# Sixteen FFN blocks by seven products in place of fourteen, sums of x in place, and another order at the end, in a two-layer decoder kernel

## The chip, the cores and the metric

The kernel runs on one core of one Trainium2 chip. The metric is the device time of one execution in microseconds, as the median of several runs. TensorE (PE in the rows, with PEld for its weight loads), VectorE (DVE), ScalarE (ACT) and GpSimd (POOL) each take their own instructions in order; SyncE (SP) issues the loads and stores.

## The reference

```python
D_MODEL, SEQ, D_FF = 1024, 512, 2752

def swiglu(h, w_gate, w_up, w_down):
    return (jax.nn.silu(h @ w_gate) * (h @ w_up)) @ w_down

for layer in range(2):
    x = x + 0.5 * swiglu(rmsnorm(x, ffn1_norm[layer]), ffn1 weights of the layer)
    h = rmsnorm(x, mix_norm[layer])
    if layer == 0:
        x = x + parallel_s5_stickbreak(h, ...)
    else:
        x = x + short_conv_mixer(h, ...)
    x = x + 0.5 * swiglu(rmsnorm(x, ffn2_norm[layer]), ffn2 weights of the layer)
return rmsnorm(x, final_norm)
```

All is float32. The four FFNs, numbered 0 to 3, are most of the work. The mixers are not touched by the change.

## The kernel before, in words

x lies transposed in eight tiles of 128 rows (features) by 512 columns (sequence). TensorE multiplies float32 by three products in a shorter format: each operand is split into an upper part ("hi", a cast on ScalarE) and a lower part ("lo", a subtraction on VectorE), and hi·hi, lo·hi and hi·lo are added (`mm3`, lines 309 to 311).

**Weights.** They are units of 128 x 1024 in an order fixed by the list of steps. A unit is loaded to one of three "raw" buffers, cast to "whi" (`cut_hi`, L212) and completed with "wlo" (`cut_lo`, L218); `refill` then issues the load three units on. `drive` runs the steps: for a unit it first calls `advance`, which cuts the unit that is two ahead, then issues the unit's products and what follows them (`after`). A unit with `split_before` skips `advance`. So the order of the calls is the order in each engine's queue.

**An FFN** has 21 blocks of 128 hidden columns and a tail of 64. It goes in three parts ("thirds"): the blocks of a part are computed, and then the down products of these blocks, in eight units (dt = 0 to 7), are added to x (L547). A plain block is two units (gate and up) over the eight tiles of x, 24 matmuls of 512 columns each. Its evacuation is, for the gate, t (L489), the silu s on ScalarE (L491) and s times rb (L492); for the up unit, the product (L501), its cast "hhi" (L502) and its lower part "hlo" (L503). rb is the reciprocal root of the norm. The tail block's lines are 512 to 520.

**Seven products.** In the second and third part of FFNs 1, 2 and 3 a block is computed by seven products of half size in place of eight, in the manner of Strassen and Winograd: gate and up weights, in halves of the 1024 features, against x in halves of features and sequence. This takes 84 matmuls of 256 columns (`seven_products`, L681), sums of the weights (`mate_pieces`, L279 to L284, "s" with parts "shi" and "slo") and sums of x. For x, `seven_x` (L615) forms "xn", x times norm times rb, two operations for each i of 0 to 3. Before, this follows blocks 3 to 6, and the sums and casts stand beside the down units: `seven_sums` (L633 to L640) makes four sums in scratch tiles "t", casts them ("thi") and casts parts of xn ("bhi"); `seven_lower` (L648 to L652) makes the lower parts "tlo" and "blo". With tail, the first part has 7 blocks and the tail, the others 7 each. FFN 0 is plain throughout.

**The end.** The last part of FFN 3 has its own function, `last_down`: the down units run twice, once for each half of the sequence (256 columns), 16 units in all. After a unit: x is updated (L764), and on ScalarE squared for the final norm (L773) and scaled (L774), and the squares are added (L776). During the second half, the first half's root is computed (`first_sums`, `norm_diag`, `first_bcast`) and its rows are stored.

Of the kernel before, what the change touches and what calls it, by code (L numbers as in the profile page):

```python
# [8 lines left out]
F32 = mybir.dt.float32  # L9
F32R = mybir.dt.float32r  # L10
I32 = mybir.dt.int32
AF = mybir.ActivationFunctionType
ALU = mybir.AluOpType
# [8 lines left out]
TAIL = 21  # L22
PLAIN_THIRDS = [list(range(0, 8)), list(range(8, 15)), list(range(15, 22))]
SEVEN_THIRDS = [list(range(0, 7)) + [TAIL], list(range(7, 14)), list(range(14, 21))]
SEVEN = (1, 2, 3)
# [118 lines left out]
class Trunk:  # L144
# [321 lines left out]
    def ffn(self, n, nxt):  # L466

        st = self
# [86 lines left out]

        for third in range(3):
# [7 lines left out]
            for f in [] if seven else sorted(thirds[third], key=lambda f: (f != TAIL or third == 0, f if f != TAIL else 4.5)):  # L564
                keep = []
                if f == TAIL:
                    st.steps.append(Unit(gu[n, 2 * f], 1024, st.over_x("A", keep), evac_tail(keep)))
                    continue
                g, u = evac_gate(keep, f), evac_up(keep, f)
                if f == 0:  # L570
                    early, keep0 = [g, u], keep
                    g = u = None
                    if n == st.first_ffn:
                        g, u = (lambda r=r: [st.feed_sq(st.first_norm, k) for k in r] for r in (range(4), range(4, 8)))
                elif f == 1:
                    def ug(g=g, u=u, keep=keep):
                        st.norm_bcast()
                        for kp, (gg, uu) in ((keep0, early), (keep, (g, u))):
                            pu = kp.pop()
                            gg()  # L580
                            kp.append(pu)
                            uu()
                    g, u = st.norm_sums, ug
                pair = [Unit(gu[n, 2 * f], 1024, st.over_x("A", keep), g), Unit(gu[n, 2 * f + 1], 1024, st.over_x("A", keep), u)]
                if f == 0 and n == st.first_ffn:
                    pair[0].products = lambda u, p=pair, k=keep: st.over_x_two("A", p, [k, k])
                    pair[1].products = lambda u: None
                st.steps += pair
                if n in SEVEN and 3 <= f < 7:
                    st.steps.append(lambda i=f - 3: st.seven_x(n, i))  # L590
# [26 lines left out]

    def seven_parts(self, dt):

        sums, lower = {0: (0, 1), 2: (2,), 3: (3,)}, {1: 0, 2: 1, 4: 2, 5: 3}  # L620
        return [lambda: self.seven_lower(lower[dt])] * (dt in lower) + [
            lambda i=i: self.seven_sums(i) for i in sums.get(dt, ())]

    def seven_sums(self, i):


        nc, v, x = self.nc, self.nc.vector, self.xn[i]
        b11, b12, b21, b22 = (x[:, c:c + 256] for c in range(0, 1024, 256))
        t = self.fp.tile([128, 512], F32, tag="t", name="t12", bufs=2), self.fp.tile([128, 512], F32, tag="s", name="t34", bufs=2)
        l, r = slice(0, 256), slice(256, 512)  # L630
        hi = [self.xgp.tile([128, 512], F32R, tag="xhi", name="thi") for _ in range(2)]
        b = self.sp7.tile([128, 768], F32R, tag="bhi", name="bhi", bufs=4)
        v.tensor_tensor(t[0][:, l], b12, b11, ALU.subtract)  # L633
        nc.scalar.copy(b[:, 0:256], b11)
        v.tensor_tensor(t[0][:, r], b22, t[0][:, l], ALU.subtract)
        nc.scalar.copy(hi[0], t[0])
        v.tensor_tensor(t[1][:, l], b22, b12, ALU.subtract)
        v.tensor_tensor(t[1][:, r], b21, t[0][:, r], ALU.subtract)
        nc.scalar.copy(hi[1], t[1])
        nc.scalar.copy(b[:, 256:768], x[:, 512:1024])  # L640
        self.t7[i], self.b7[i] = [t, hi], [b]

    def seven_lower(self, i):
        v, x = self.nc.vector, self.xn[i]
        t, hi = self.t7[i]
        lo = [self.xgp.tile([128, 512], F32R, tag="xlo", name="tlo") for _ in range(2)]
        for a, h, o in zip(t, hi, lo):
            v.tensor_tensor(o, a, h.bitcast(F32), ALU.subtract)  # L648
# [4 lines left out]
        self.t7[i], self.b7[i] = (hi, lo), (b, o)  # L653
# [6 lines left out]
    def seven_products(self, f, u):  # L660
# [31 lines left out]
        t1, t2, t3, t4 = (total(j) for j in range(4))  # L692
# [46 lines left out]
    def last_down(self, units):  # L739
# [20 lines left out]

        def after(dt, h):
            c = slice(h * H, h * H + H)
            x = st.x[dt][:, c]
            v.scalar_tensor_tensor(x, ps[dt, h], 0.5, x, ALU.mult, ALU.add)  # L764
# [10 lines left out]
            if 0 < dt < NK - 1:  # L775
                v.tensor_tensor(st.acc[:, c], st.acc[:, c], sq, ALU.add)  # L776

# [57 lines left out]
        extra = {0: [first_sums], 1: [lambda: st.norm_diag(2)], 2: [first_bcast]}  # L835
        for k in range(NK):
            extra.setdefault(3 + k // 2, []).append(lambda k=k: first_out(k))
        for h in range(2):
            for dt, u in enumerate(units[h]):
                u.products = lambda u, dt=dt, h=h: products(u, dt, h)  # L840
                todo = [lambda dt=dt, h=h: after(dt, h)]
                if h:
                    todo = extra.get(dt, []) + todo if dt == 0 else todo + extra.get(dt, [])
# [1104 lines left out]
```

## Time and profile before

| | |
|---|---|
| median of 3 runs | 1835.75 us (1835.69 to 1835.79) |
| profiled execution, its own time | 1837.11 us |
| its span, first to last instruction | 1835.4 us |
| granted TensorE clock, mean | 0.995 |
| busy: PE, PEld | 99%, 86% |
| busy: DVE, ACT, POOL | 71%, 40%, 6% |
| moved by DMA | 201.64 MB, mean 110 GB/s |

The rows shown later come from the profiled execution; its own time stands beside its span because the time around the span is not in any row. Busy time of PE is counted from instructions that overlap, so for what one matmul takes, look at the time of a stage and the number of its matmuls. A mean share says nothing of a single stage: the stages have different limits.

### The profile page before, as it was taken

Reading aid. Unit: us, or ns where it says so; the run is one execution under the profiler, and the core shown is the slowest. Engines: PE = TensorE matmul, PEld = TensorE weight load, DVE = VectorE, ACT = ScalarE, POOL = GpSimd, SP = SyncE. Lnnn points to the kernel's source line nnn. Section 1 sums busy time; section 2 is a strip of 40 time slices with the busy share of each in tenths; the row PEclk is TensorE's granted clock in tenths of the full one; section 3 lists DMA queues with packets and bytes.
Section 4 is the critical chain, followed back from the end, with each engine's and each line's share of the span. In section 5 each row is a group of like instructions: output and inputs, shape, how many; then the busy total and the mean of one; then the engine's idle time right before and its main releaser. Section 6 shows DMA issues by size and latency. Waiting matters only on the chain.

```text
span 1835.4 us, 25692 instructions
## 1 busy us (share of the span) xinstructions
PE 1808.5 (99%) x10006; PEld 1575.2 (86%) x10006; DVE 1299.5 (71%) x2157; ACT 741.4 (40%) x1117; POOL 116.5 (6%) x238
## 2 busy tenths in 40 slices
PE   9999999999989999999999999999999999999997
PEld 8887888888877788999988899898888888898997
DVE  6757777656787567967855689596655556895975
ACT  5322323334786334534443344244222333452444
POOL 0290000110000200000010000001100100000001
PEclk9999999999989999999999999999999999999999
DMA  4334444456411233332332333333333223333334
GB/s 162 122 98 139 122 131 145 134 169 214 144 47 47 81 104 92 115 100 96 108 103 89 95 111 98 98 114 94 95 101 104 92 86 99 104 102 105 103 105 127
DMA packets 82457, 201.64 MB, mean 110 GB/s; under 512 B 20816, under 2 KB 31072, under 8 KB 82336
## 3 DMA queue, kind: packets, MB, share of 16 engines
q1 hardware_dynamic: 82160, 199.97, 35.1%
q8 instruction: 78, 1.28, 0.3%
q14 instruction: 43, 0.35, 0.1%
q10 hardware_dynamic: 144, 0.03, 0.0%
q0 software_dynamic: 32, 0.01, 0.0%
HBM read 184.12 MB, written 12.58 MB: 107 GB/s over the span
## 4 chain that ended last, share of the span: by engine, by line
PE 87%; DVE 4%; POOL 3%; ACT 3%; issue 2%; DMA 1%; SPq 0%; DVEq 0%; POOLq 0%; ACTq 0%
PE ps_A L681 23%; PE ps_A L309 11%; PE ps_A L310 11%; PE ps_A L311 11%; PE ps_mm L309 8%; PE ps_mm L310 8%; PE ps_mm L311 8%; DVE wlo L218 1%; ACT whi L212 1%; PE ps_mm L1653 1%; PE ps_mm L1655 1%; PE ps_mm L1654 1%; PE ps_A L1248 0%; PE ps_A L1250 0%; PE ps_A L1249 0%
## 5 line engine op out<-in xcount | busy, mean ns | idle before, releaser
L218 DVE TENSOR_TENSOR wlo<-raw,whi 128x1024 fp32r<-128x1024 f32 (+1 forms) x290 | 355.8, 1227 | 131.9 <-ACT whi L212 131.4
L212 ACT CAST whi<-raw 128x1024 fp32r<-128x1024 f32 (+1 forms) x290 | 295.0, 1020 | 267.5 <-PE ps_mm L311 120.5
L309 PE MATMUL ps_A<-xhi,whi 128*128 128x512 f32 x896 | 350.5, 391 | 0.0
L310 PE MATMUL ps_A<-xhi,wlo 128*128 128x512 f32 x896 | 349.1, 390 | 1.4 <-DVE wlo L218 1.4
L311 PE MATMUL ps_A<-xlo,whi 128*128 128x512 f32 x896 | 348.9, 389 | 0.1
L309 PE MATMUL ps_mm<-hhi,whi 128*128 128x512 f32 (+1 forms) x672 | 256.7, 382 | 1.1 <-DVE x L764 1.1
L310 PE MATMUL ps_mm<-hhi,wlo 128*128 128x512 f32 (+1 forms) x672 | 256.3, 381 | 0.4 <-DVE wlo L218 0.4
L311 PE MATMUL ps_mm<-hlo,whi 128*128 128x512 f32 (+1 forms) x672 | 256.1, 381 | 0.0
L310 PEld LDWEIGHTS ps_A<-xhi,wlo 128*128 128x128 f32 x896 | 168.4, 188 | 36.9 <-DVE wlo L218 2.3
L309 PEld LDWEIGHTS ps_A<-xhi,whi 128*128 128x128 f32 x896 | 168.4, 188 | 35.6 <-issue 0.8
L311 PEld LDWEIGHTS ps_A<-xlo,whi 128*128 128x128 f32 x896 | 168.3, 188 | 35.7 <-DVE xlo L367 0.5
L309 PEld LDWEIGHTS ps_mm<-hhi,whi 128*128 128x128 f32 x672 | 127.1, 189 | 25.5 <-issue 1.7
L310 PEld LDWEIGHTS ps_mm<-hhi,wlo 128*128 128x128 f32 x672 | 127.2, 189 | 24.4 <-DVE wlo L218 0.6
L311 PEld LDWEIGHTS ps_mm<-hlo,whi 128*128 128x128 f32 x672 | 127.0, 189 | 24.0
L681 PE MATMUL ps_A<-thi,shi 128*128 128x256 f32 x504 | 142.6, 283 | 0.0
L681 PE MATMUL ps_A<-thi,slo 128*128 128x256 f32 x504 | 142.6, 283 | 0.0
L681 PE MATMUL ps_A<-tlo,shi 128*128 128x256 f32 x504 | 142.6, 283 | 0.0
L547 DVE SCALAR_TENSOR_TENSOR x<-ps_mm,x 128x512 f32<-128x512 f32 x88 | 60.4, 689 | 76.9 <-PE ps_mm L311 72.7
L269 DVE TENSOR_TENSOR slo<-s,shi 128x512 fp32r<-128x512 f32 (+1 forms) x126 | 107.7, 863 | 1.6
L681 PEld LDWEIGHTS ps_A<-thi,shi 128*128 128x128 f32 x504 | 96.8, 192 | 0.0
L681 PEld LDWEIGHTS ps_A<-thi,slo 128*128 128x128 f32 x504 | 96.8, 192 | 0.0
L681 PEld LDWEIGHTS ps_A<-tlo,shi 128*128 128x128 f32 x504 | 96.8, 192 | 0.0
(396 smaller groups left out, 3315.7 us busy)
## 6 DMA issues: line engine op xcount, KB each, us to landing
raw<-gu SPq DMA_DIRECT2D x170, 512.0 KB, 3.5
raw<-dn SPq DMA_DIRECT2D x96, 448.0 KB, 3.3
raw<-sci SPq DMA_DIRECT2D x24, 512.0 KB, 3.5
raw<-ab SPq DMA_DIRECT2D x16, 512.0 KB, 3.6
raw<-dn SPq DMA_DIRECT2D x8, 512.0 KB, 3.6
raw<-abo SPq DMA_DIRECT2D x8, 512.0 KB, 3.5
raw<-sco SPq DMA_DIRECT2D x8, 512.0 KB, 3.4
x<-xT SPq DMA_DIRECT2D x8, 256.0 KB, 5.1
```

The source lines that it names most:

```text
L212: self.nc.scalar.copy(u.hi[:, : u.cols], u.raw[:, : u.cols])
L218: (engine or self.nc.vector).tensor_tensor(u.lo[:, :c], u.raw[:, :c], u.hi[:, :c].bitcast(F32), ALU.subtract)
L269: v.tensor_tensor(u.s_lo[i][:, c], s[i][:, c], u.s_hi[i][:, c].bitcast(F32), ALU.subtract)
L309: nc.tensor.matmul(ps, whi, xhi, start=start and i == 0, stop=False)
L310: nc.tensor.matmul(ps, wlo, xhi, start=False, stop=False)
L311: nc.tensor.matmul(ps, whi, xlo, start=False, stop=stop and i == n - 1)
L547: nc.vector.scalar_tensor_tensor(x, keep[0], 0.5, x, ALU.mult, ALU.add)
L681: nc.tensor.matmul(ps, a, m, start=first and k == 0 and n == 0, stop=k == 3 and n == 2, skip_group_check=True)
L1653: nc.tensor.matmul(X["ps"], u.hi[:, c], hi, start=k == 0, stop=False)
L1654: nc.tensor.matmul(X["ps"], u.lo[:, c], hi, start=False, stop=False)
L1655: nc.tensor.matmul(X["ps"], u.hi[:, c], lo, start=False, stop=k == 3)
```

## The change

Three things are done together.

1. The parts of FFNs 1, 2 and 3 become 5 blocks and the tail, 8, and 8. So 16 blocks are computed by seven products, and the depths of the down units become 17, 24 and 24 matmuls in place of 23, 21 and 21. The end's 16 units get 24 matmuls of 256 columns in place of 21, and 512 KB of weights in place of 448.
2. `seven_x` now also casts the parts of xn ("bhi") on ScalarE, and is called after the units (2, gate), (2, up), (3, up) and (4, gate). The sums are made in place in xn, with "blo" ahead of them, after the tail, (3, gate), (4, up) and the first down unit. The casts "thi" and the lower parts "tlo" stay beside the down units. The tail moves between blocks 2 and 3.
3. In `last_down`, the cast of a unit's weights is issued ahead of the products two units before it; after the products come the update of x, then the lower part and the load, then square and scaling. The root's steps stand ahead of the update.

```diff
-SEVEN_THIRDS = [list(range(0, 7)) + [TAIL], list(range(7, 14)), list(range(14, 21))]
+SEVEN_THIRDS = [list(range(0, 5)) + [TAIL], list(range(5, 13)), list(range(13, 21))]
...
+        def seven_x(f, j):
+            if n not in SEVEN:
+                return []
+            x, t = (lambda i: [lambda: st.seven_x(n, i)]), (lambda i: [lambda: st.seven_sums(i)])
+            return {(2, 0): x(0), (2, 1): x(1), (TAIL, 0): t(0), (3, 0): t(1), (3, 1): x(2), (4, 0): x(3), (4, 1): t(2)}.get((f, j), [])
...
-            for f in [] if seven else sorted(thirds[third], key=lambda f: (f != TAIL or third == 0, f if f != TAIL else 4.5)):
+            for f in [] if seven else sorted(thirds[third], key=lambda f: (f != TAIL or third == 0, f if f != TAIL else 2.5)):
...
+                    st.steps += seven_x(f, 0)
...
-                st.steps += pair
-                if n in SEVEN and 3 <= f < 7:
-                    st.steps.append(lambda i=f - 3: st.seven_x(n, i))
+                for j in range(2):
+                    st.steps.append(pair[j])
+                    st.steps += seven_x(f, j)
...
+        b = self.sp7.tile([128, 768], F32R, tag="bhi", name="bhi", bufs=4)
+        self.nc.scalar.copy(b[:, 0:256], self.xn[i][:, 0:256])
+        self.nc.scalar.copy(b[:, 256:768], self.xn[i][:, 512:1024])
+        self.b7[i] = [b]
 
     def seven_sums(self, i):
...
         v.tensor_tensor(o[:, 0:256], x[:, 0:256], b[:, 0:256].bitcast(F32), ALU.subtract)
         v.tensor_tensor(o[:, 256:768], x[:, 512:1024], b[:, 256:768].bitcast(F32), ALU.subtract)
-        self.t7[i], self.b7[i] = (hi, lo), (b, o)
+        self.b7[i] = (b, o)
+        q11, q12, q21, q22 = (x[:, c:c + 256] for c in range(0, 1024, 256))
+        v.tensor_tensor(q11, q12, q11, ALU.subtract)
+        v.tensor_tensor(q12, q22, q12, ALU.subtract)
+        v.tensor_tensor(q22, q22, q11, ALU.subtract)
+        v.tensor_tensor(q21, q21, q22, ALU.subtract)
+
+    def seven_parts(self, dt):
+        return [lambda: self.seven_sums(3)] * (dt == 0) + [lambda: self.seven_lower(dt - 1)] * (1 <= dt <= 4) + [
+            lambda: self.seven_upper(dt)] * (dt < 4)
+
+    def seven_upper(self, i):
+        hi = [self.xgp.tile([128, 512], F32R, tag="xhi", name="thi") for _ in range(2)]
+        for j in range(2):
+            self.nc.scalar.copy(hi[j], self.xn[i][:, j * 512:(j + 1) * 512])
+        self.t7[i] = hi
+
+    def seven_lower(self, i):
+        hi = self.t7[i]
+        lo = [self.xgp.tile([128, 512], F32R, tag="xlo", name="tlo") for _ in range(2)]
+        for j in range(2):
+            self.nc.vector.tensor_tensor(lo[j], self.xn[i][:, j * 512:(j + 1) * 512], hi[j].bitcast(F32), ALU.subtract)
+        self.t7[i] = (hi, lo)
...
-        t1, t2, t3, t4 = (total(j) for j in range(4))
+        t1, t3, t4, t2 = (total(j) for j in range(4))
...
+        def first_part(u):
+            if st.split < len(st.units):
+                st.cut_hi(st.split)
+
+        def second_part():
+            n = st.split
+            if n < len(st.units):
+                st.cut_lo(n)
+                st.refill(n)
...
-        extra = {0: [first_sums], 1: [lambda: st.norm_diag(2)], 2: [first_bcast]}
+        extra = {}
...
+        early = {0: [first_sums], 1: [lambda: st.norm_diag(2)], 2: [first_bcast]}
...
-                u.products = lambda u, dt=dt, h=h: products(u, dt, h)
-                todo = [lambda dt=dt, h=h: after(dt, h)]
-                if h:
-                    todo = extra.get(dt, []) + todo if dt == 0 else todo + extra.get(dt, [])
+                u.split_before = True
+                u.products = lambda u, dt=dt, h=h: (first_part(u), products(u, dt, h))
+                todo = early.get(dt, []) * h + [lambda dt=dt, h=h: update(dt, h), second_part, lambda dt=dt, h=h: after(dt, h)]
+                todo += extra.get(dt, []) * h
```

How this moves the instructions is seen at three places. The first is ScalarE in FFN 1, from the silu of block 2's gate on. Before:

```order
L491 ACTIVATE s<-t 128x512
L212 CAST whi<-raw 128x1024
L502 CAST hhi<-s 128x512
L212 CAST whi<-raw 128x1024
L491 ACTIVATE s<-t 128x512
```

Now:

```order
L491 ACTIVATE s<-t 128x512
L626 CAST bhi<-xn 128x256
L627 CAST bhi<-xn 128x512
L212 CAST whi<-raw 128x1024
L502 CAST hhi<-s 128x512
L626 CAST bhi<-xn 128x256
L627 CAST bhi<-xn 128x512
L212 CAST whi<-raw 128x1024
L513 ACTIVATE s<-t 64x512
```

Two casts of xn now stand ahead of each weight cast, and the tail's silu follows block 2. The second place is VectorE over the same steps. Before:

```order
L489 TENSOR_TENSOR t<-ps_A,rb 128x512
L492 TENSOR_TENSOR s<-s,rb 128x512
L218 TENSOR_TENSOR wlo<-raw,whi 128x1024
L501 TENSOR_TENSOR s<-ps_A,s 128x512
L503 TENSOR_TENSOR hlo<-s,hhi 128x512
L218 TENSOR_TENSOR wlo<-raw,whi 128x1024
```

Now, and on to the tail's second lower part, the sum made after it and the weights behind that:

```order
L489 TENSOR_TENSOR t<-ps_A,rb 128x512
L492 TENSOR_TENSOR s<-s,rb 128x512
L623 SCALAR_TENSOR_TENSOR xn<-x_82,norms,rb 128x512
L623 SCALAR_TENSOR_TENSOR xn<-x_93,norms,rb 128x512
L218 TENSOR_TENSOR wlo<-raw,whi 128x1024
L501 TENSOR_TENSOR s<-ps_A,s 128x512
L503 TENSOR_TENSOR hlo<-s,hhi 128x512
```

```order
L520 TENSOR_TENSOR both<-s,hi_5955 64x512
L636 TENSOR_TENSOR blo<-xn,bhi 128x256
L637 TENSOR_TENSOR blo<-xn,bhi 128x512
L640 TENSOR_TENSOR xn<-xn 128x256
L641 TENSOR_TENSOR xn<-xn 128x256
L642 TENSOR_TENSOR xn<-xn 128x256
L643 TENSOR_TENSOR xn<-xn 128x256
L218 TENSOR_TENSOR wlo<-raw,whi 128x1024
```

xn moved ahead of wlo after block 2's units, and a sum of six operations stands ahead of the wlo that follows the tail. The third place is VectorE at the first units of the end. Before:

```order
L218 TENSOR_TENSOR wlo<-raw,whi 128x896
L764 SCALAR_TENSOR_TENSOR x_82<-ps_A,x_82 128x256
L218 TENSOR_TENSOR wlo<-raw,whi 128x896
L764 SCALAR_TENSOR_TENSOR x_85<-ps_A,x_85 128x256
L776 TENSOR_TENSOR acc<-acc,sq 128x256
```

Now:

```order
L773 SCALAR_TENSOR_TENSOR x_82<-ps_A,x_82 128x256
L218 TENSOR_TENSOR wlo<-raw,whi 128x1024
L773 SCALAR_TENSOR_TENSOR x_85<-ps_A,x_85 128x256
L218 TENSOR_TENSOR wlo<-raw,whi 128x1024
L789 TENSOR_TENSOR acc<-acc,sq 128x256
```

The update of x and the lower part of the weights two units on have changed places.

## Rows read from the trace of the kernel before

**Rows 1.** The profile page, part 1: busy us, share of the span, instructions.

```profile
PE 1808.5 (99%) x10006; PEld 1575.2 (86%) x10006; DVE 1299.5 (71%) x2157; ACT 741.4 (40%) x1117; POOL 116.5 (6%) x238
```

**Rows 2.** Windows, FFN 1: length, busy PE, PEld, DVE, ACT, POOL; clock, DMA, GB/s.

```profile
634.50:694.60 60.10, 60.10 (x265) 49.44 (x264) 37.58 (x47) 22.95 (x30) 0.52 (x1) 1.00 0.33 98
736.30:806.90 70.60, 70.60 (x590) 70.59 (x589) 64.50 (x107) 33.80 (x53) 0.00 (x0) 1.00 0.36 114
806.90:845.00 38.10, 38.10 (x171) 31.54 (x170) 19.78 (x25) 9.89 (x11) 0.00 (x0) 1.00 0.35 106
```

**Rows 3.** Timeline, DVE, plain blocks of FFN 1: start, length, operation, idle before.

```profile
644.45 1.23 DVE L218 TENSOR_TENSOR wlo<-raw,whi 128x1024 fp32r<-128x1024 f32 x1 [0.26 <-ACT whi L212]
645.59 0.68 DVE L489 TENSOR_TENSOR t<-ps_A,rb 128x512 f32<-128x512 f32 x1
647.03 0.69 DVE L492 TENSOR_TENSOR s<-s,rb 128x512 f32<-128x512 f32 x1 [0.76 <-ACT s L491]
...
656.72 0.69 DVE L501 TENSOR_TENSOR s<-ps_A,s 128x512 f32<-128x512 f32 x1 [0.52 <-PE ps_A L311]
658.10 0.69 DVE L503 TENSOR_TENSOR hlo<-s,hhi 128x512 fp32r<-128x512 f32 x1 [0.69 <-ACT hhi L502]
658.71 1.41 DVE L615 SCALAR_TENSOR_TENSOR xn<-x,norms,rb 128x512 f32<-128x512 f32 x2
```

**Rows 4.** Timeline, DVE, the tail of FFN 1, and sums beside its down units.

```profile
673.04 0.68 DVE L512 TENSOR_TENSOR t<-ps_A,rb 64x512 f32<-64x512 f32 x1 [0.91 <-PE ps_A L311]
...
676.59 0.69 DVE L520 TENSOR_TENSOR both<-s,hi 64x512 fp32r<-64x512 f32 x1 [0.68 <-ACT hi L518]
...
700.62 0.42 DVE L633 TENSOR_TENSOR t<-xn 128x256 f32<-128x256 f32 x1
701.07 0.42 DVE L635 TENSOR_TENSOR t<-xn,t 128x256 f32<-128x256 f32 x1
...
709.14 0.42 DVE L651 TENSOR_TENSOR blo<-xn,bhi 128x256 fp32r<-128x256 f32 x1
709.48 0.68 DVE L652 TENSOR_TENSOR blo<-xn,bhi 128x512 fp32r<-128x512 f32 x1
```

**Rows 5.** Timeline, ACT, FFN 1.

```profile
657.97 1.05 ACT L212 CAST whi<-raw 128x1024 fp32r<-128x1024 f32 x1
...
702.73 0.61 ACT L640 CAST bhi<-xn 128x512 fp32r<-128x512 f32 x1
703.25 0.40 ACT L634 CAST bhi<-xn 128x256 fp32r<-128x256 f32 x1
```

**Rows 6.** Timeline, block 2's first matmul in FFNs 1 and 3, and a wlo of FFN 3.

```profile
634.46 0.39 PE L309 MATMUL ps_A<-xhi,whi 128*128 128x512 f32 x1
...
1494.31 0.39 PE L309 MATMUL ps_A<-xhi,whi 128*128 128x512 f32 x1
...
1503.74 1.23 DVE L218 TENSOR_TENSOR wlo<-raw,whi 128x1024 fp32r<-128x1024 f32 x1 [0.26 <-ACT whi L212]
```

**Rows 7.** Windows, the two halves of the end, columns as in rows 2.

```profile
1775.10:1797.60 22.50, 21.27 (x171) 20.45 (x169) 12.99 (x21) 11.35 (x20) 0.00 (x0) 1.00 0.43 123
1797.60:1826.00 28.40, 23.93 (x179) 23.02 (x179) 17.56 (x38) 13.43 (x26) 4.38 (x5) 0.94 0.35 107
```

**Rows 8.** Timeline, ACT and DVE, one turn of the end's units.

```profile
1783.41 0.92 ACT L212 CAST whi<-raw 128x896 fp32r<-128x896 f32 x1
...
1784.36 1.09 DVE L218 TENSOR_TENSOR wlo<-raw,whi 128x896 fp32r<-128x896 f32 x1 [0.81 <-ACT whi L212]
1785.37 0.42 DVE L764 SCALAR_TENSOR_TENSOR x<-ps_A,x 128x256 f32<-128x256 f32 x1
...
1786.55 0.92 ACT L212 CAST whi<-raw 128x896 fp32r<-128x896 f32 x1
```

**Rows 9.** Timeline, PE in the end's second half; the window behind it, columns as in rows 2.

```profile
1811.26 0.78 PE L801 MATMUL ps_A<-diag,ones 128*128 128x256 f32 x2 [1.94 <-DVE diag L442]
...
1812.60:1816.00 3.40, 3.40 (x18) 3.40 (x17) 1.76 (x3) 1.92 (x4) 1.80 (x3) 0.50 0.51 140
```

More of the change, by code (lines that the diff above doesn't have):

```diff
@@ L616, in seven_x @@
                 self.xn[i][:, j * 512:(j + 1) * 512], self.x[k], self.norms[:, (0, 2, 3, 5)[n], k:k + 1], self.rb, ALU.mult, ALU.mult)
[L618 to L622, printed above, removed]
+        b = self.sp7.tile([128, 768], F32R, tag="bhi", name="bhi", bufs=4)
+        self.nc.scalar.copy(b[:, 0:256], self.xn[i][:, 0:256])
+        self.nc.scalar.copy(b[:, 256:768], self.xn[i][:, 512:1024])
+        self.b7[i] = [b]
     def seven_sums(self, i):
[L627 to L643, printed above, removed]
         v, x = self.nc.vector, self.xn[i]
[L645 to L648, printed above, removed]
         b = self.b7[i][0]
@@ L759, in products, with update @@
             ])
+        def update(dt, h):
+            c = slice(h * H, h * H + H)
+            x = st.x[dt][:, c]
+            v.scalar_tensor_tensor(x, ps[dt, h], 0.5, x, ALU.mult, ALU.add)
         def after(dt, h):
@@ L763, in after @@
             x = st.x[dt][:, c]
-            v.scalar_tensor_tensor(x, ps[dt, h], 0.5, x, ALU.mult, ALU.add)
             if dt == 0 and h == 0:
```

## The prediction

> **What bounds the kernel now.** I read the shares of busy time first, then the windows by stage, then the order of time on VectorE (DVE) and ScalarE (ACT). In the shares, TensorE (PE) is busy for 99% of the span and VectorE for 71% [rows 1]. The windows of FFN 1 (of 0 to 3) say the same stage by stage: PE is busy for all of 60.1 us of plain blocks, all of 70.6 us of seven-product blocks and all of 38.1 us of down units, while the granted clock is 1.00 [rows 2]. So between the prologue and the end, time is what the matmuls take. VectorE has 37.58 of 60.10 us of work beside the plain blocks and 64.50 of 70.60 beside the seven-product blocks [rows 2]. The end is different: there PE waits, 22.5 and 28.4 us for two halves of equal matmuls [rows 7].
>
> **1. Blocks, removed and added.** A down stage of 168 matmuls of 512 columns takes 38.1 us, so one takes 0.2268 us [rows 2]. A plain block is 48 of them, 10.89 us. Seven blocks by seven products took 70.6 us, 10.09 each [rows 2]. Six blocks change form: 6 x 0.80 = **4.8 us less**.
> The down units change depth. In FFNs 1 and 2 the sum is the same, 8 x (23 + 21 + 21) = 8 x (17 + 24 + 24) = 520 matmuls. In the last FFN the third part lies in the end stage, costed below; the other two lose 48 and gain 24: 24 x 0.2268 = **5.4 us less**.
> The loads grow from 448 to 512 KB where a down unit grows, and the DMA engines are busy for 0.33 to 0.43 of these stages [rows 2, 7]; I cost that at nothing. If it were not covered, PE would wait for "raw" ahead of the casts.
>
> **2. The end.** Before, a loop through two engines sets the pace: the cast of the next weights on ACT (0.92), their lower part on VectorE (1.09), behind it the update of x (0.42), and only then the square and the scaling on ACT, with the next cast behind them. From cast to cast it is 1783.41 to 1786.55, 3.14 us [rows 8]. The 21 matmuls of a unit need 21 x 0.12 = 2.52 (10.09 / 84 = 0.12 for one of 256 columns). The diff issues the cast ahead of the products and the update ahead of the lower part. Then a unit's lower part is done some 0.42 + 1.23 + 0.25 = 1.9 us after the matmuls two units ahead of it, and the unit between takes 24 x 0.12 = 2.88: a second to spare in every three, so PE sets the pace. 16 x 2.88 = 46.1, and I allow 0.8 for each of the two norm steps among them, as long as the one shown [rows 9]: 47.7 against 22.5 + 28.4 = 50.9 [rows 7]: **3.2 us less**. Bounds: if the loop stayed, with 1024 columns (1.05 and 1.23 in place of 0.92 and 1.09) it takes 3.4 a unit, 54.4, or 3.5 us more than now; at best the norm steps are free, 4.8 less.
>
> **3. The first part of each FFN: the work that moves.** Before, the products x times norm (two "xn" operations, 1.41 us [rows 3]) stood after blocks 3 to 6 and their sums beside the down units. Now all of the products and three of the four sums stand between the five plain blocks and the tail. Three things change the queues. The casts "bhi" of xn come right behind xn on ACT, ahead of the next unit's weight cast, so that cast now waits for VectorE. The lower part of the weights waits for that cast. And the next evacuation stands behind it on VectorE. Both engines take their instructions in order, so the pieces add up, where before the cast ran beside xn.
> The pieces, from start to start: a gate's evacuation, t to s and past it, 1.44 + 0.60 = 2.04; an up's, 1.38 + 0.61 = 1.99; the weights' lower part 1.14 [rows 3]. The tail's, 3.55 + 0.61 = 4.16. A sum: "blo" 0.34 + 0.60, then four in-place operations, three at 0.34 and one at 0.45 since the last needs the third, 2.41 [rows 4]. From xn's start to the start of the lower part: 1.41, the second "bhi" 0.52, the cast 1.05 [rows 3, 5], and hand-overs of 0.1 in all: 3.08. For the 768 columns of the first down units I take cast and lower part 0.26 and 0.28 shorter (two steps of 128 columns, at the 0.13 and 0.14 between 896 and 1024 [rows 3, 5, 8]).
> VectorE comes to block 2 at 645.59, as before [rows 3], because nothing changes ahead of it. From there:
> gate 2 with xn 2.04 + 3.08 + 1.14 = 6.26; up 2 with xn 6.21; tail with sum 4.16 + 2.41 + 1.14 = 7.71; gate 3 with sum 5.59; up 3 with xn 1.99 + 2.82 + 0.86 = 5.67; gate 4 with xn 5.72; up 4 until "hlo" is written 1.38 + 0.69 = 2.07. The sum is 39.2, so block 4's hlo is ready at 684.8.
> PE starts block 2 at 634.46 [rows 6]. Seven units of 24 matmuls are 38.1 us, and the first down unit, which now holds only five blocks and the tail, wants this hlo at its 15th matmul, 3.2 us later: 675.7. **It is 9.1 us late**, and PE waits that long in all: some 4 us in pieces for "wlo" at the four units before, and 5 us in one piece within the first down unit. The unit time of PE is 5.44, and six of the seven steps above are longer; VectorE's 63% share hid this, since in a chain it waits as long as it works. Before, PE lost 0.2 us in this stage (60.1 against 264 x 0.2268 = 59.9), so 8.9 more. In the last FFN VectorE takes up the same weights 9.43 us after PE's start, here 9.99 (644.45 - 634.46) [rows 3, 6], so 0.56 less: 8.5; FFN 2 runs like it. Together **25.9 us more**. After the first down unit, VectorE's part of a unit (lower part, update, two lower parts of the sums, 2.7 us) is below PE's 17 x 0.2268 = 3.86, so nothing is left of the lag. Bounds: 2 us either way for hand-overs.
>
> **4. The clock after the wait.** At the end, PE waited 1.94 us before 1811.26, and from 1812.6 its granted clock was 0.50, the level of 1.2 GHz, for 3.4 us, which cost half of them [rows 9]. The new wait of 5 us within the first down unit is longer, so I take one such stretch behind each: 3 x 1.7 = **5.1 us more**. Bounds: nothing, or two such stretches behind each. The Trainium skill ("TensorE: Matmul & The Clock Gate", HAM oscillation) says that a wait which PE spends idle brings the clock to half and that every such wait pays again; that rule speaks against this change. The row agrees with it. By the rule all three waits pay, as in my sum; without it the sum would be 5.1 us smaller.
>
> **The sum.** -4.8 - 5.4 - 3.2 + 25.9 + 5.1 = +17.6 us. The profiled execution took 1837.11 (span 1835.4); the median of the runs shown is 1835.75, and I add the sum to that: **1853.4 us**.
>
> **The rivals.**
> *The casts of xn hold nothing up (faster).* Then a step with xn is 4.59 for a gate (2.04 + 1.41 + 1.14) in place of 6.26, and so on four times: 6.7 us less of chain, a lag of 2.4, and 2.2 + 1.8 + 1.8 = 5.8 us in place of 25.9, with no wait as long as the one before the clock fell: 1835.75 - 13.4 + 5.8 = 1828.2. For it: VectorE is idle for 22 us of that stage [rows 2]. Against it: ACT's order in the changed program, with both bhi ahead of the cast. The change breaks even where the lags come to 13.4 us, 4.5 for each FFN. Chance 0.08.
> *Half a lag.* A hand-over or a cast that I count is hidden, the lag comes to that 4.5, and the clock holds: 1835 or so. Chance 0.05.
> *The clock holds.* The waits come as worked out, but no stretch at half: 1848.3. Chance 0.22.
> *The clock costs double*, two stretches behind each wait: 1858.5. Chance 0.15.
> *The end does not do what the diff says*, because the loop stays with larger weights: 6.7 above the forecast, 1860.1. Against it: update and lower part have changed places on VectorE. Chance 0.05.
> *Operations run to their end.* In the timeline, hlo starts at 658.10, takes 0.69, and xn starts at 658.71, ahead of its end [rows 3]; I used 0.6 between starts. If the in-place sums and their neighbours did not overlap, some 25 starts per FFN come 0.08 later, 6 us in all: 1859.4. The Trainium skill ("VectorE: DVE Perf Modes", The DRAIN you can't avoid) says that the next operation waits until the pipe is empty; the row disagrees. Chance 0.03.
> The forecast has the remaining 0.42.
>
> **How the numbers follow.** The forecast, the clock's two sides and the last two rivals all lie between 1846 and 1861 (1853.4 less 5.1 and 2, plus 5.1 and 2): 0.87 of the chance, and that is the range. About 0.2%, 3.7 us, is what a measurement of this kernel can tell from no change. Faster by more: the first rival and part of the second, 0.09. Within: 0.03. Slower: 0.88.
>
> **What would show it.** In the changed profile: seven-product stages of 80.7 us for eight blocks with PE full (part 1); sixteen end units at 2.9 us and no wait on wlo there (part 2); in the first part of FFNs 1 to 3, the weight cast waiting on xn or bhi, PE waiting for wlo at 1 to 2 us a piece and once for hhi and hlo for 5 us inside the first down unit (part 3); a granted clock below 1.00 just behind that (part 4). I am wrong if PE is full in the windows of plain blocks, or if the weight cast stands ahead of bhi's wait there.

## The result, and the profile after

| | before | after |
|---|---|---|
| median | 1835.72 us (1835.56 to 1835.79, 4 runs) | 1857.12 us (1855.33 to 1858.54, 4 runs) |
| ratio | | 1.0116, interval 1.0100 to 1.0132 |
| profiled execution, its span | 1837.11, 1835.4 us | 1857.9, 1856.2 us |
| granted TensorE clock, mean | 0.995 | 0.991 |

The change makes the kernel slower by 21.4 us; 17.6 were forecast, and the time lies in the range. The busy line of the page has hardly moved against [rows 1], and by it alone nobody would look for a loss:

```profile
PE 1813.3 (98%) x10246; PEld 1583.9 (85%) x10246; DVE 1329.0 (72%) x2217; ACT 757.8 (41%) x1141; POOL 117.9 (6%) x238
```

The windows by stage show it. Columns are as in [rows 2]. The first four are FFN 1: seven plain units, eight down units, eight seven-product blocks, eight down units; the last two are the halves of the end.

```profile
634.50:677.60 43.10, 39.94 (x170) 31.14 (x168) 29.19 (x44) 17.98 (x26) 0.52 (x1) 1.00 0.21 64
677.60:714.80 37.20, 32.98 (x138) 26.53 (x137) 30.77 (x50) 15.80 (x23) 0.00 (x0) 0.95 0.37 110
714.80:795.40 80.60, 80.60 (x673) 80.60 (x672) 73.44 (x121) 39.25 (x61) 0.00 (x0) 1.00 0.36 110
795.40:839.00 43.60, 43.60 (x195) 36.09 (x194) 20.58 (x25) 10.55 (x11) 0.00 (x0) 1.00 0.32 100
...
1798.90:1822.10 23.20, 23.20 (x194) 23.06 (x193) 14.72 (x23) 13.91 (x23) 0.00 (x0) 1.00 0.49 144
1822.10:1846.90 24.80, 24.70 (x205) 24.30 (x204) 17.92 (x35) 12.39 (x23) 5.65 (x5) 1.00 0.45 138
```

The parts with eight blocks do what was forecast: 80.6 us, and PE full. The end falls from 50.9 to 23.2 + 24.8 = 48.0 us. The first part of FFN 1 holds 304 matmuls, which at 0.2268 us take 68.95; it takes 43.10 + 37.20 = 80.3, so 11.3 are lost. FFN 2 loses 10.9 (windows of 42.50 and 37.30) and FFN 3 12.0 (43.70 and 37.30): 34.2, of which 0.2 were lost before. With the terms of parts 1 and 2 it closes: -4.8 - 5.4 - 2.9 + 34.0 = +20.9, and the spans differ by 20.8.

Where PE waits in the first part of FFN 1, and what its first matmuls do behind the last wait (timeline of PE after the change; the bracket is the idle time before and what ended it):

```profile
666.26 0.50 PE L310 MATMUL ps_A<-xhi,wlo 128*128 128x512 f32 x1 [1.88 <-DVE wlo L218]
...
684.93 0.78 PE L309 MATMUL ps_mm<-hhi,whi 128*128 128x512 f32 x1 [4.22 <-ACT hhi L502]
...
687.63 0.63 PE L310 MATMUL ps_mm<-hhi,wlo 128*128 128x512 f32 x1
688.06 0.55 PE L311 MATMUL ps_mm<-hlo,whi 128*128 128x512 f32 x1
```

PE waits for wlo at four units (0.52, 0.40, 1.88 and 0.23) and once, inside the first down unit, for block 4's hhi (4.22) and then hlo. Behind that, two matmuls start 0.43 us apart in place of 0.23. The window of that stretch gives the granted clock 0.50, the 1.2 GHz level:

```profile
685.00:688.40 3.40, 3.40 (x8) 2.67 (x9) 3.30 (x8) 2.99 (x6) 0.00 (x0) 0.50 0.29 98
1562.20:1569.00 6.80, 6.03 (x14) 4.72 (x15) 6.01 (x13) 4.27 (x7) 0.00 (x0) 0.50 0.30 78
```

Such a stretch lies behind the hhi wait of each of FFNs 1 to 3: 3.4 us in the first two, 6.8 in FFN 3 (second row). A fourth, of 3.4 us, lies in FFN 3 alone behind the wait for wlo at block 4 (1.88 us, before 1544.32):

```profile
1545.10:1548.50 3.40, 3.40 (x9) 2.64 (x8) 2.69 (x6) 1.55 (x2) 0.00 (x0) 0.51 0.41 116
```

PE is later by it, and so waits for hhi behind it 3.34 us (before 1562.97) in place of 4.22 in the other two FFNs.

Why wlo is late is read on ScalarE and VectorE over block 2 (timelines after the change):

```profile
646.43 0.64 ACT L491 ACTIVATE s<-t 128x512 f32<-128x512 f32 x1 [1.96 <-DVE t L489]
648.49 0.41 ACT L626 CAST bhi<-xn 128x256 fp32r<-128x256 f32 x1 [1.42 <-DVE xn L623]
...
649.68 1.05 ACT L212 CAST whi<-raw 128x1024 fp32r<-128x1024 f32 x1
```

```profile
645.65 0.69 DVE L489 TENSOR_TENSOR t<-ps_A,rb 128x512 f32<-128x512 f32 x1
...
647.71 1.41 DVE L623 SCALAR_TENSOR_TENSOR xn<-x,norms,rb 128x512 f32<-128x512 f32 x2
650.76 1.23 DVE L218 TENSOR_TENSOR wlo<-raw,whi 128x1024 fp32r<-128x1024 f32 x1 [1.64 <-ACT whi L212]
651.90 0.69 DVE L501 TENSOR_TENSOR s<-ps_A,s 128x512 f32<-128x512 f32 x1
...
663.27 0.42 DVE L640 TENSOR_TENSOR xn<-xn 128x256 f32<-128x256 f32 x1
663.73 0.43 DVE L641 TENSOR_TENSOR xn<-xn 128x256 f32<-128x256 f32 x1
...
664.65 0.42 DVE L643 TENSOR_TENSOR xn<-xn 128x256 f32<-128x256 f32 x1
664.99 1.22 DVE L218 TENSOR_TENSOR wlo<-raw,whi 128x1024 fp32r<-128x1024 f32 x1
...
684.91 0.69 DVE L503 TENSOR_TENSOR hlo<-s,hhi 128x512 fp32r<-128x512 f32 x1 [0.69 <-ACT hhi L502]
```

ScalarE is free after the silu, but the cast it could make waits behind bhi, bhi waits for xn on VectorE, and VectorE then stands idle for 1.64 us until the cast is done. From gate 2's evacuation at 645.65 to up 2's at 651.90 it is 6.25 us (forecast 6.26), against the 24 x 0.2268 = 5.44 that PE needs.

### The profile page after: what moved, and what is told of

Its sections match the earlier page's. It is cut to its first block, busy times and chain, and to the rows that moved or that the text cites. A ratio compares the mean times of both kernels' runs of the same rounds, so it can differ in the third digit from the quotient of the medians.

```text
span 1856.2 us, 26254 instructions
## 1 busy us (share of the span) xinstructions
PE 1813.3 (98%) x10246; PEld 1583.9 (85%) x10246; DVE 1329.0 (72%) x2217; ACT 757.8 (41%) x1141; POOL 117.9 (6%) x238
## 3 DMA queue, kind: packets, MB, share of 16 engines
q8 instruction: 80, 1.31, 0.3%
## 4 chain that ended last, share of the span: by engine, by line
PE 80%; DVE 8%; ACT 4%; POOL 3%; issue 3%; DMA 1%; SPq 0%; DVEq 0%; POOLq 0%; ACTq 0%
PE ps_A L690 26%; PE ps_A L309 8%; PE ps_A L311 8%; PE ps_A L310 8%; PE ps_mm L309 8%; PE ps_mm L310 7%; PE ps_mm L311 7%; DVE wlo L218 2%; ACT whi L212 1%; DVE xn L623 1%; PE ps_mm L1678 1%; PE ps_mm L1679 1%; PE ps_mm L1680 1%; ACT s L491 1%; DVE s L501 1%
## 5 line engine op out<-in xcount | busy, mean ns | idle before, releaser
L218 DVE TENSOR_TENSOR wlo<-raw,whi 128x1024 fp32r<-128x1024 f32 (+2 forms) x284 | 348.3, 1227 | 112.2 <-ACT whi L212 111.7
L212 ACT CAST whi<-raw 128x1024 fp32r<-128x1024 f32 (+2 forms) x284 | 290.9, 1025 | 311.5 <-PE ps_mm L311 126.3
L310 PE MATMUL ps_A<-xhi,wlo 128*128 128x512 f32 x800 | 313.7, 392 | 9.8 <-DVE wlo L218 9.8
L309 PE MATMUL ps_A<-xhi,whi 128*128 128x512 f32 x800 | 313.8, 392 | 0.7 <-ACT xhi L361 0.4
L311 PE MATMUL ps_A<-xlo,whi 128*128 128x512 f32 x800 | 312.5, 391 | 0.1
L310 PEld LDWEIGHTS ps_A<-xhi,wlo 128*128 128x128 f32 x800 | 150.5, 188 | 46.1 <-DVE wlo L218 15.0
L690 PE MATMUL ps_A<-thi,shi 128*128 128x256 f32 x576 | 163.0, 283 | 0.0
L690 PE MATMUL ps_A<-thi,slo 128*128 128x256 f32 x576 | 163.0, 283 | 0.0
L690 PE MATMUL ps_A<-tlo,shi 128*128 128x256 f32 x576 | 163.0, 283 | 0.0
L311 PEld LDWEIGHTS ps_mm<-hlo,whi 128*128 128x128 f32 x672 | 127.4, 190 | 24.8 <-DVE hlo L503 0.9
L269 DVE TENSOR_TENSOR slo<-s,shi 128x1024 fp32r<-128x1024 f32 x144 | 123.4, 864 | 1.8
```

The lines of the kernel that those rows point to most:

```text
L212: self.nc.scalar.copy(u.hi[:, : u.cols], u.raw[:, : u.cols])
L218: (engine or self.nc.vector).tensor_tensor(u.lo[:, :c], u.raw[:, :c], u.hi[:, :c].bitcast(F32), ALU.subtract)
L269: v.tensor_tensor(u.s_lo[i][:, c], s[i][:, c], u.s_hi[i][:, c].bitcast(F32), ALU.subtract)
L309: nc.tensor.matmul(ps, whi, xhi, start=start and i == 0, stop=False)
L310: nc.tensor.matmul(ps, wlo, xhi, start=False, stop=False)
L311: nc.tensor.matmul(ps, whi, xlo, start=False, stop=stop and i == n - 1)
```

## The experiments

The kernel before was run beside them on the same chip: 1835.30 us in the median for the first four runs, 1835.72 for the last two.

**The casts one unit later.** The changed kernel, with the two bhi casts in a function of their own, called a unit after their xn. ScalarE's weight cast then no longer stands behind them.

```diff
-return {(2, 0): x(0), (2, 1): x(1), (TAIL, 0): t(0), (3, 0): t(1), (3, 1): x(2), (4, 0): x(3), (4, 1): t(2)}.get((f, j), [])
+return {(2, 0): x(0), (2, 1): b(0) + x(1), (TAIL, 0): b(1) + t(0), (3, 0): t(1), (3, 1): x(2),
+        (4, 0): b(2) + x(3), (4, 1): b(3) + t(2)}.get((f, j), [])
...
+    def seven_b(self, i):
         b = self.sp7.tile([128, 768], F32R, tag="bhi", name="bhi", bufs=4)
```

> The changed kernel with one thing moved: the casts bhi of xn are issued one unit later, so that no weight cast stands behind an xn that has just been issued. Theory (ScalarE's hold on the weight cast is most of the lag): four steps per FFN lose 3.08 - 1.32 = 1.76 us each, 7.0 in all. With the sums as the changed kernel's trace shows them (2.75 us each in place of 2.41) the chain from 645.65 ends near 679.1, 3.4 us after PE wants it, against 9.9 in the changed kernel; the clock does not fall, since no single wait reaches 2 us. The first parts then lose some 9 us in all where they lose 34: 1832 us (1829 to 1836). Rival 1 (the lag is VectorE's plain amount of work in this stage, and the casts only fill its idle time): no more than 1 us per FFN comes back, 1853 or above. Rival 2 (the wait inside the first down unit comes from the shorter down units, not from the queues): the pieces at the plain units go, the 4.2 us wait and the slow clock stay, 1845 or so.

Measured: 1832.33 us, ratio to before 0.9977 (0.9966 to 0.9988); 24.8 us below the change. The first part of FFN 1, and block 2 on ScalarE and VectorE in this kernel:

```profile
634.00:673.60 39.60, 38.98 (x169) 31.30 (x168) 29.77 (x45) 17.04 (x25) 0.52 (x1) 1.00 0.25 71
673.60:706.40 32.80, 31.37 (x137) 25.37 (x136) 29.64 (x47) 15.77 (x25) 0.00 (x0) 1.00 0.40 123
```

```profile
646.47 1.04 ACT L212 CAST whi<-raw 128x1024 fp32r<-128x1024 f32 x1
...
647.21 1.41 DVE L625 SCALAR_TENSOR_TENSOR xn<-x,norms,rb 128x512 f32<-128x512 f32 x2
648.53 1.22 DVE L218 TENSOR_TENSOR wlo<-raw,whi 128x1024 fp32r<-128x1024 f32 x1
```

The cast runs beside xn, wlo follows xn with no idle time, and the step is 4.5 us (645.16 to 649.67) in place of 6.25. The three first parts lose 3.5 + 2.95 + 2.95 = 9.4 us in place of 34.2, and no stretch of them is at half the clock; the longest wait of PE that the first part of FFN 1 shows is 1.43 us. That no wait would reach 2 us was too weak a ground for this, since the clock had fallen behind 1.94 us in the kernel before [rows 9]. The same instructions and the same work: the position of eight short casts in each FFN is what most of the loss hangs on, the slow clock behind the waits included.

**The end alone.** The kernel before with the third part of the change only, so with 21 matmuls in an end unit. Its edit is the change's own for `last_down`:

```diff
-                todo = [lambda dt=dt, h=h: after(dt, h)]
...
+                u.split_before = True
+                u.products = lambda u, dt=dt, h=h: (first_part(u), products(u, dt, h))
+                todo = early.get(dt, []) * h + [lambda dt=dt, h=h: update(dt, h), second_part, lambda dt=dt, h=h: after(dt, h)]
```

> The kernel before with part 3 alone: the end's order as in the changed kernel, 14 blocks by seven products, 21 matmuls a unit. Theory (the end's loop through two engines was what PE waited for, and the new order breaks it): 16 units x 2.52 = 40.3 plus about 1.9 for the norm steps, as the changed kernel's 48.0 less 16 x 2.88 = 46.1, makes 42.2 in place of 50.9: 1827 us (1826 to 1828.5). Rival (the end is bound by the loads, 448 KB a unit, or by VectorE, and the changed kernel is only as fast as its longer units let it be): a unit stays near the 2.88 us of the changed kernel's, 48 us, 1833.

Measured: 1828.42 us, ratio 0.9954 (0.9936 to 0.9971). The two halves, and ScalarE over one turn:

```profile
1774.40:1795.10 20.70, 20.48 (x171) 20.26 (x169) 13.78 (x23) 13.00 (x23) 0.00 (x0) 1.00 0.47 137
1795.10:1817.80 22.70, 22.04 (x180) 21.43 (x179) 16.98 (x35) 11.69 (x23) 5.38 (x5) 1.00 0.45 137
```

```profile
1783.88 0.92 ACT L212 CAST whi<-raw 128x896 fp32r<-128x896 f32 x1
...
1786.46 0.92 ACT L212 CAST whi<-raw 128x896 fp32r<-128x896 f32 x1
```

From cast to cast it is 2.58 us where it was 3.14 [rows 8], near the 2.52 that 21 matmuls need. The end takes 43.4 us, 7.5 less than before and 1.2 more than expected. The loop is not all of it: the first half gains 1.8 us (22.5 to 20.7) and the second 5.7 (28.4 to 22.7). In its second half the kernel before shows two more waits of PE at the norm steps, beside the one of 1.94 us [rows 9]:

```profile
1802.29 0.60 PE L784 MATMUL ps_A<-ones,sq 128*128 128x1 f32 x4 [1.05 <-ACT sq L773]
...
1806.58 0.36 PE L309 MATMUL ps_mm<-hhi,whi 128*128 128x256 f32 x1 [1.06 <-DVE x L764]
```

The three are 4.05 us, and the stretch at half the clock behind them cost 1.7. In this kernel's second half PE waits at most 0.28 us at a time and the granted clock is 1.00. The run breaks the loop and moves the norm steps at once, so what either gives alone is not shown. This part of the change gains by itself.

**The moved sums alone.** The kernel before (14 blocks, old end) with the second part of the change: its table of calls for `seven_x` and `seven_sums`, the sums in place, the tail between blocks 2 and 3.

```diff
-                if n in SEVEN and 3 <= f < 7:
-                    st.steps.append(lambda i=f - 3: st.seven_x(n, i))
+                for j in range(2):
+                    st.steps.append(pair[j])
+                    st.steps += seven_x(f, j)
```

> The kernel before with part 2 alone: 14 blocks by seven products and the old end, but xn, bhi and the sums where the changed kernel has them, and the tail between blocks 2 and 3. Theory (the place of the sums makes the loss, whatever the number of blocks): the waits ahead of the fourth block's units stay as in the changed kernel, some 4 us per FFN, and the lag is worked off in blocks 5 and 6 at some 2.2 us a unit with 1 or 2 us more of waits, so 5 to 6 us per FFN and a slow stretch of the clock behind at most some of them: 1853 us (1849 to 1857). Rival (the loss belongs to the first part's shortening to five blocks; with seven there is time enough): within 3 us of the kernel before, 1836 to 1839.

Measured: 1855.14 us, ratio 1.0099 (1.0083 to 1.0115). FFN 1's plain stage, and the longest of PE's waits in it:

```profile
633.30:700.00 66.70, 62.59 (x266) 48.95 (x265) 46.08 (x67) 27.05 (x38) 0.52 (x1) 1.00 0.30 87
```

```profile
665.03 0.50 PE L310 MATMUL ps_A<-xhi,wlo 128*128 128x512 f32 x1 [1.90 <-DVE wlo L218]
```

264 matmuls take 66.7 us where they took 60.1 [rows 2]. The three plain stages take 6.8, 6.1 and 6.2 us more than the 59.9 of their matmuls, 19.2 in all with the rounding, and that is about the loss: the medians lie 19.8 us apart, the profiled spans 17.8. So the new place of x's operations is enough for it, without more blocks and without the new end.

**PE kept busy in the long wait.** The changed kernel with 16 more matmuls in the first down unit of FFNs 1 to 3, whose result is not read.

```diff
+                if n in SEVEN and third == 0 and dt == 0:
+                    st.mm3(ps, p[:4], stop=False)
+                    idle = st.bank("A")
+                    for _ in range(EXTRA):
+                        nc.tensor.matmul(idle, u.hi[:, 0:128], st.h[0][0], start=True, stop=True)
+                    st.mm3(ps, p[4:], start=False, stop=False)
...
```

> The changed kernel with 16 added matmuls of 512 columns, whose product nobody reads, in the first down unit of FFNs 1 to 3 between its fourth and its fifth block: 3.6 us of work for PE in the wait of 4.2 us there. It shows what the half clock costs. Theory (the clock falls because PE waits there, and each stretch at half costs 1.7 us): the slow stretches behind the wait go, four such stretches of 3.4 us in the changed kernel's trace, so 5 to 6.8 us less: 1851 us (1850 to 1853). Rival 1 (the fall comes from the pieces of waits at the units before, 1.9 us at the fourth block): the stretches stay and the time is unchanged, 1857. Rival 2 (time at half clock costs nothing here, since VectorE's queue is what is waited for): the stretches go and the time stays, 1857.

Measured: 1852.05 us, ratio 1.0083 (1.0067 to 1.0098), so 5.1 us below the change by the medians. Block 4's products in the down unit (this kernel's lines stand one lower), and one window behind the wait for wlo at block 4 in FFN 2:

```profile
684.80 0.50 PE L310 MATMUL ps_mm<-hhi,whi 128*128 128x512 f32 x1 [0.57 <-ACT hhi L503]
...
686.57 0.39 PE L311 MATMUL ps_mm<-hhi,wlo 128*128 128x512 f32 x1
686.79 0.39 PE L312 MATMUL ps_mm<-hlo,whi 128*128 128x512 f32 x1
```

```profile
1016.60:1020.00 3.40, 3.40 (x9) 2.67 (x8) 2.58 (x7) 1.56 (x2) 0.00 (x0) 0.50 0.41 116
```

hhi comes as late as it did (684.80 against 684.93), but the matmuls behind it start 0.22 apart, and the granted clock is 1.00 from 684 to 690. More matmuls make the kernel faster. Two stretches at half the clock are left, in FFNs 2 and 3, behind waits of 1.9 us at block 4; they cost little, since the time comes out of the wait behind them: in FFN 2 block 4's products start at 1034.77, 0.14 after the cast of hhi ends. What this run cannot give is the clock's price to a tenth: the runs of one kernel lie up to 6 us apart here (1825.42 to 1831.00 in the run of the end alone).

**The waits filled.** 16 blocks and the new end, with x's operations put into the times in which VectorE waits for ScalarE: one xn operation between t and s of a gate and between product and hlo of an up unit, from block 0 on; blo likewise at blocks 3 and 4; bhi a unit after its xn; the in-place sums after block 3's units and the first two down units.

```diff
                 nc.scalar.activation(s, t, AF.Silu)
+                fill(f, 0)
                 nc.vector.tensor_tensor(s, s, st.rb, ALU.mult)
...
                 nc.scalar.copy(hi, s)
+                fill(f, 1)
                 nc.vector.tensor_tensor(lo, s, hi.bitcast(F32), ALU.subtract)
```

> Sixteen blocks and the changed end, but xn and blo stand on VectorE where it waited for ScalarE: one xn operation (0.66) or one pair blo (0.94) between a gate's t and its s, between an up unit's product and its hlo, and twice in the tail, waits of 0.69 to 0.76 each; from blocks 0 and 1 on, whose waits were empty too. The casts bhi come one unit after their xn, ahead of that unit's silu or hhi, where ScalarE waited. Two in-place sums stand after block 3's units and two at the first two down units. Theory (the lag is a matter of places, not of work): a step is 3.2 us, and 5.2 where a sum stands, so VectorE catches up within the stage and PE does not wait for it: 1835.3 - 4.8 - 5.4 - 2.9 = 1822 us (1821 to 1825). Rival (VectorE's work itself does not fit into five blocks and a tail): at least half of the lag of the run with later casts stays, 1827 or more.

Measured: 1823.58 us (1822.09 to 1824.94), ratio to before 0.9933 (0.9920 to 0.9947). It beats both kernels. Windows of FFN 1, and VectorE at block 2:

```profile
632.70:671.00 38.30, 38.28 (x169) 31.42 (x168) 33.61 (x51) 19.54 (x30) 0.52 (x1) 1.00 0.28 83
671.00:701.80 30.80, 30.80 (x137) 25.51 (x137) 26.07 (x41) 13.42 (x19) 0.00 (x0) 1.00 0.41 119
```

```profile
643.81 0.69 DVE L504 TENSOR_TENSOR t<-ps_A,rb 128x512 f32<-128x512 f32 x1
644.41 0.74 DVE L643 SCALAR_TENSOR_TENSOR xn<-x,norms,rb 128x512 f32<-128x512 f32 x1
645.25 0.69 DVE L508 TENSOR_TENSOR s<-s,rb 128x512 f32<-128x512 f32 x1
646.20 1.23 DVE L218 TENSOR_TENSOR wlo<-raw,whi 128x1024 fp32r<-128x1024 f32 x1 [0.25 <-ACT whi L212]
```

From t to s it is 1.44 us with an xn in between, as it is without one [rows 3]: that xn costs nothing. The step is 3.53 us (643.81 to 647.34), the stage 69.1 for 68.95 of matmuls, although VectorE is busier in it (33.61 of 38.30) than in the changed kernel.

**The sums where they were.** 16 blocks and the new end, with the sums in scratch tiles beside the down units as before, and one xn pair after (2, up), the tail, (3, up) and (4, up). Its table of calls, against the changed kernel's; the functions that make the sums are those of the kernel before:

```diff
-return {(2, 0): x(0), (2, 1): x(1), (TAIL, 0): t(0), (3, 0): t(1), (3, 1): x(2), (4, 0): x(3), (4, 1): t(2)}.get((f, j), [])
+return {(2, 1): x(0), (TAIL, 0): x(1), (3, 1): x(2), (4, 1): x(3)}.get((f, j), [])
```

> Sixteen blocks and the changed end with the sums where the kernel before had them: xn after the units (2, up), the tail, (3, up) and (4, up), the scratch sums, casts and lower parts beside the down units. It shows what the moved sums are worth by themselves. Theory (the move into the plain units costs more than it frees): the first down stage is 136 x 0.2268 = 30.8 us while VectorE had 33 us of work beside it before, less some 1.7 for its narrower weights, so PE waits 1 to 5 us per FFN there for VectorE, and nowhere else: 1826 to 1837, 1833 likeliest, over 15 us below the changed kernel. Rival (with the shorter down stage the sums there would cost as much as among the plain units, so that the move was needed): 1850 or above.

Measured: 1846.82 us, ratio 1.0060 (1.0046 to 1.0074), below the rival and well above the forecast: a miss. The down stage of FFN 1, and ScalarE, VectorE and PE at its third unit:

```profile
670.70:706.50 35.80, 32.74 (x137) 26.43 (x136) 28.50 (x52) 14.81 (x25) 0.00 (x0) 0.95 0.30 87
```

```profile
689.19 0.62 ACT L644 CAST thi<-t 128x512 fp32r<-128x512 f32 x1 [7.12 <-DVE t L643]
...
690.91 0.83 ACT L212 CAST whi<-raw 128x768 fp32r<-128x768 f32 x1
...
688.28 0.42 DVE L641 TENSOR_TENSOR t<-xn 128x256 f32<-128x256 f32 x1
688.74 0.42 DVE L643 TENSOR_TENSOR t<-xn,t 128x256 f32<-128x256 f32 x1
689.08 0.42 DVE L645 TENSOR_TENSOR t<-xn 128x256 f32<-128x256 f32 x1
...
691.77 0.96 DVE L218 TENSOR_TENSOR wlo<-raw,whi 128x768 fp32r<-128x768 f32 x1 [1.94 <-ACT whi L212]
...
693.48 0.76 PE L309 MATMUL ps_mm<-hhi,whi 128*128 128x512 f32 x1 [2.72 <-DVE x L547]
```

The plain stage is free of loss here (38.4), but the down stage loses 5.0 us (some 1.7 of it by the clock, whose mean is 0.95 there) and the seven-product stage 2.8 (83.4 for 80.6). It is the same pattern in another place: the weight cast stands behind the casts of the sums, which ScalarE could only start after 7.12 us without work; behind it come wlo and the update of x, for which PE waits. I had priced these sums by how they ran beside down units of 23 matmuls, and the shorter units of 17 no longer cover them.

## Why the prediction was right, and where it was off

**Part 1** held. Eight blocks in 80.6 us are 10.08 each, and a down stage of 192 matmuls takes 43.6: -4.8 and -5.4 as worked out.

**Part 2** held: -2.9 for -3.2. A unit takes 2.88 us from cast to cast, PE's own time, and the loop through the engines is gone. ScalarE and VectorE in one turn after the change:

```profile
1806.21 1.03 ACT L212 CAST whi<-raw 128x1024 fp32r<-128x1024 f32 x1
...
1809.09 1.03 ACT L212 CAST whi<-raw 128x1024 fp32r<-128x1024 f32 x1
...
1805.02 0.42 DVE L773 SCALAR_TENSOR_TENSOR x<-ps_A,x 128x256 f32<-128x256 f32 x1 [1.31 <-PE ps_A L311]
```

VectorE now waits 1.31 us for PE in a turn, where before it was PE that waited. The sum came out, but its account of the time before was incomplete: at the loop's 3.14 us a unit the first half would have taken 25.1 us, and it took 22.5 [rows 7]; in the second, the rows show three waits at the norm steps (4.05 us) and a slow stretch behind them (1.7) that are not in the end's new order, beside the loop.

**Part 3** had the mechanism right, and the first experiment shows it: with the casts out of the way, three quarters of the loss is gone (24.8 of 34.2 us, the slow clock's part with it). The term was mis-sized by some 3 us: with 5.1 taken off for the clock, it is 34.0 - 5.1 = 28.9 for 25.9. The steps came out one by one as

| step | forecast | measured |
|---|---|---|
| gate 2, up 2 with xn | 6.26, 6.21 | 6.25, 6.17 |
| tail with sum | 7.71 | 8.17 |
| gate 3 with sum | 5.59 | 5.85 |
| up 3, gate 4 with xn | 5.67, 5.72 | 5.69, 5.76 |
| up 4 until hlo is written | 2.07 | 2.06 |

Block 4's hlo is ready at 684.91 + 0.69 = 685.60, 9.9 us late where 9.1 were forecast. The two steps that were too short are those with a sum: I took the first two steps between the in-place operations at 0.34 us from start to start, and all three are 0.46 (663.27 to 664.65). That is 0.25 us for each sum, 0.5 for each FFN. Another 0.2 lie in the tail's step, half in its evacuation (4.26 from 658.07 to 662.33, forecast 4.16) and half behind the weights' lower part (1.25 from 664.99 to 666.24, forecast 1.14). Together it is 0.7 us for each FFN, 2.2 in all. The other 0.8 us of the term I leave open; it is within the scatter of the runs. The waits that the rows show (3.0 us for wlo, 4.2 for hhi) come to less than the lag, since an idle time counts from an end that is modelled.

**Part 4** held: 5.1 us by the run that keeps PE busy, 5.1 forecast. That the two agree to the tenth is luck. The count was less even than forecast: behind the three hhi waits lie two stretches of 3.4 us and one of 6.8, a fourth place in FFN 3 has one more, and the run that keeps PE busy still has two of 3.4; its times spread over 1.0 us and those of the changed kernel over 3.2. The Trainium skill ("TensorE: Matmul & The Clock Gate", HAM oscillation) says that each such wait pays again; the stretches behind the three hhi waits agree with that, while of the three waits of 1.9 us for wlo at block 4 only the one in FFN 3 has one behind it. The run in which PE works through the hhi wait has none there, so that wait is their cause.

**The rivals.** That the casts hold nothing up fell: bhi waits 1.42 us for xn and the weight cast behind it. Made true by the first experiment, it gives 1832.3 and not the 1828.2 I gave it. The sum of that rival has a slip: it takes 1.67 us off each of the four steps with xn, but for the two with 768 columns it is 2.82 - 1.41 = 1.41, so 0.5 less for each FFN. With the 2.2 us of the steps with a sum, its 5.8 us become 9.6; 9.4 were lost, 0.2 of them before. That the clock holds fell too, and that it costs double holds for FFN 3 alone. That the end's loop stays fell by the 2.88. That operations run to their end is true of the in-place sums (0.42 long, 0.46 apart) and not of their neighbours (1.14 from a wlo of 1.23 to the next), so it is worth 1.5 us and not 6. The Trainium skill ("VectorE: DVE Perf Modes", The DRAIN you can't avoid) says that the next operation does not start until the pipe is empty, and adds that one which is not held starts earlier; the rival took the first half alone. The starts behind the end of the one ahead, in the in-place sums, and the earlier starts of the others agree with the two halves; whether "held" there covers these sums, no run here shows.

What the change was worth without its one bad order: the waits-filled kernel has its blocks, its depths and its end, and comes out 33.5 us below it. Against the kernel before, the end alone gives about 7 of the 12 us gained there; the deeper use of seven products gives the rest, but these two were timed on different chips and their difference of 5 us is not far above the scatter.

## What to carry to other kernels

Where two engines that work in order hand tiles to and fro, an operation that waits for the other engine must not stand ahead of one that could run at once: here eight short casts for each FFN, ahead of the weight casts, turned work that ran side by side into a chain, and cost 25 us with the clock that fell behind PE's waits. A busy share of 63% says nothing of such a chain; walk the steps from start to start and set the longest against the time of the engine that should set the pace. New work goes into the waits that the timeline already shows (between a product and its cast's return), where 0.7 us of it cost nothing, and a move from one stage to the next is priced against that stage's new length.

## What the runs showed of the hardware that I had not expected

Operations on VectorE of 128 x 256 elements take 0.42 us each, whatever stands ahead. Independent ones start 0.34 us apart; one that reads what the one just ahead wrote starts 0.46 behind it (688.28 to 688.74, then 689.08, in the kernel with the old sums), and so does one that writes over what the one ahead read (663.27 to 664.19 in the changed kernel). Whether a wait in the program or the engine itself holds them was not tried.

A wait of 1.9 us was enough for a stretch at the 1.2 GHz level (at block 4, in FFN 3 of the changed kernel and in FFNs 2 and 3 of the kernel with PE kept busy), but not always: the one of 1.88 us at 666.26 in FFN 1 of the changed kernel has none behind it, and that window is at 1.00. What tells the two cases apart is open.
